# One core, a float32 mixer block: token-major products made 512 columns wide, gated linear attention in 64x64 tiles, and a new static order

## The chip, the cores and the metric

The kernel runs on one core of a Trainium2 chip. The metric is device time in microseconds (us) of one execution; lower is better. Engines are named as in the profile: PE is TensorE (matrix products and transposes), PEld its weight loads, DVE is VectorE, ACT is ScalarE, POOL is GpSimd, SP is SyncE, which issues most of the loads.

## The reference

Two layers, each with four token mixers that read the same normalised input: multi-head latent attention, neighbourhood attention, a long convolution (Hyena) and bidirectional gated linear attention (GLA). There are 256 context tokens and 256 latent tokens; the last layer needs no output for the context tokens. Everything is float32.

```python
for l in range(DEPTH):                                   # DEPTH = 2, D_MODEL = 1024
    h  = rms_norm(x,  pre_g[l]) * (1.0 + scale) + shift  # scale, shift from silu(c) @ ada_w[l]
    hc = rms_norm(cx, pre_g[l]) * (1.0 + scale_c) + shift_c
    ya, yca = mla_branch(h, hc, ...)                     # low-rank latents: rms_norm(h @ w_in[:, :256]) ...
    yb, ycb = na_branch(h, hc, ...)
    yh, ych = hyena_branch(h, hc, ...)
    yg, ycg = gla_branch(h, hc, ...)
    # merge_branches, for the latent and (layer 0 only) the context stream:
    gates  = sigmoid(h @ w_in[:, merge])                 # 4 branches x 1024 channels
    merged = sum(gates[i] * ((y[i] * silu(h @ w_in[:, z[i]])) @ w_branch[l, i]) for i in range(4))
    x = x + gate * rms_norm(merged @ w_out[l], post_g[l])
```

In the GLA, for each of 4 heads (key width 64, value width 128), 2 directions and chunks of 64 tokens: `a = tril((q*exp(b-bm)) @ (k*exp(bm-b)).T)`, `o = a @ v + (q*exp(b)) @ s`, and the state `s` goes on from chunk to chunk as `s = decay * s + k_out.T @ v`.

## The kernel before, in words

**Products.** Full float32 products are made of three in the faster type `fp32r`: every operand is split into a high and a low part (`wh`, `wl` of a weight; `hh`, `hl` of the normalised input; `gh`, `gl` of a gated branch output), and `mm3` issues high x high, high x low and low x high into the same PSUM bank. Products where both operands are plain float32 (the GLA, the Fourier products of the Hyena) stand in the trace as two records each. There are two kinds of projections. Channel-major ones (`proj_chan`, PSUM tile `pc`) load a piece of weights as the stationary operand and stream the tokens: 512 columns where both streams are wanted (layer 0), 256 where only one is (most of layer 1). Token-major ones (`tok`, PSUM tiles `pj` for the merge gates and the values, `br` for the branch products; `wo` of `project_out` and `pa` of the latents are built alike) hold 128 tokens stationary and stream weights: 256 columns at a time, 224 in `pa`.

**Weights.** `piece` brings 512 KB by SP into one of 3 `raw` buffers; ACT casts it to `wh` and DVE subtracts to give `wl`, each in two halves. The pool `wp` has 4 buffers of 1024 columns for each of `wh` and `wl`. A token-major call (`w_tok`) takes two pieces (8 k-tiles of 256 columns), so that two calls' weights fit.

**GLA.** `gla_dir` works on two heads (a head pair `p`) in one direction `r`, and is called four times in a layer. It makes scores (`atp`: per 128 tokens and head one 128x128x128 product, with the other head's rows of the query tile `qp` zeroed), masks them (`at`), makes state contributions (`kv`, 64x64 tiles), and sums `go` from `at` x values and from `qp` x state (`st`, output tiles of 64 tokens, again over all 128 rows). The decay logits `lg` are plain float32 products over 32 rows.

**Latents.** `latents` normalises the `pa` result of 128 tokens, turns it with four 128x128 transposes into one PSUM tile `lat` and one more transpose into `glrp`; both come from the pool `pt`, which has two banks. ACT and DVE empty `lat` in seven steps. The pool `pa` has four banks, `pmm` has two.

**Order.** PE's order is static: `drive` runs the parts of the kernel as coroutines on a counted clock (each product adds its columns/2400), and a part that issued work for another engine asks to be resumed after so many counted microseconds from the table `WAIT` (one number for each layer). What is ready by priority goes next. The other engines' orders are chosen when the program is built. The order on all engines is fixed then; at run time an engine waits where its next instruction isn't ready.

## Time and profile before

| | before |
|---|---|
| time, median of 3 runs | 1424.36 us (1422.72 to 1428.23) |
| the profiled execution's own time | 1426.96 us |
| its span, first to last instruction | 1425.2 us |
| PE busy | 1359.8 us, 95% |
| weight loads of PE busy | 1187.0 us, 83% |
| DVE, ACT, POOL busy | 889.0, 591.3, 339.7 us |
| HBM read | 163.19 MB |

The span is what the trace shows; the execution's own time is 1.8 us longer. Busy time is the union of instruction spans; since PE's products overlap each other in the pipeline (a record lasts longer than the step to the next one), what a stream of products costs is read from the starts of rows that follow each other, not from the mean duration of one.

### The profile page before, as it was taken

The page shows a single profiled execution, that of the slowest core. Times are in us where ns is not written, and L with a number is a line of the kernel's source. Part 1 is how long each engine was busy: PE and PEld are TensorE (multiplying, and loading weights), DVE is VectorE, ACT ScalarE, POOL GpSimd, SP SyncE. Part 2 cuts the span into 40 slices and gives each one's busy share as a digit, 9 for nine tenths or more (in the row PEclk, how much of TensorE's full clock was granted, in tenths as well). Part 3 has the DMA queues.
Part 4 walks back from the last instruction along what each step waited for, and adds up shares of the span by engine and source line. Part 5 has one row for each costly group of instructions (what it writes and reads, how often), then busy time and mean ns, then how long its engine had stood idle before and what let it go on. Part 6 is the DMA issues. An engine that isn't in the chain of part 4 may idle for free.

```text
span 1425.2 us, 24774 instructions
## 1 busy us (share of the span) xinstructions
PE 1359.8 (95%) x9852; PEld 1187.0 (83%) x9852; DVE 889.0 (62%) x1638; ACT 591.3 (41%) x1266; POOL 339.7 (24%) x438
## 2 busy tenths in 40 slices
PE   6989999999999999999999999889998999999996
PEld 3867788888997776889767999778888999899896
DVE  4668654565444447764476486966667776757764
ACT  3555453333222332222354443564545345434452
POOL 2423200152330201222111203532103331132110
PEclk9989999999999999999999999989998999999998
DMA  9421213232233432323334251432233255534361
GB/s 375 162 74 53 89 60 106 89 104 75 92 117 121 148 115 89 119 89 119 118 104 134 92 176 64 153 104 82 75 121 119 90 163 199 172 103 162 105 202 66
DMA packets 54308, 171.10 MB, mean 120 GB/s; under 512 B 7342, under 2 KB 10000, under 8 KB 54192
## 3 DMA queue, kind: packets, MB, share of 16 engines
q1 hardware_dynamic: 47904, 153.31, 32.3%
q0 software_dynamic: 5376, 15.90, 3.4%
q8 instruction: 77, 1.26, 0.3%
q10 hardware_dynamic: 912, 0.31, 0.1%
q14 instruction: 39, 0.32, 0.1%
HBM read 163.19 MB, written 6.31 MB: 119 GB/s over the span
## 4 chain that ended last, share of the span: by engine, by line
PE 44%; DVE 7%; issue 3%; DMA 2%; ACT 1%; POOL 1%; DVEq 0%; POOLq 0%; ACTq 0%
PE pj L380 14%; PE pc L380 9%; PE br L380 5%; PE wo L380 3%; DVE wl L370 2%; PE sc L380 2%; PE y L380 2%; DMA raw<-in_w_in 2%; PE pt L394 2%; PE pa L380 1%; PE yc L380 1%; DMA raw<-in_w_out 1%; PE go L380 1%; ACT wh L423 0%; PE q L380 0%
## 5 line engine op out<-in xcount | busy, mean ns | idle before, releaser
L370 DVE TENSOR_TENSOR wl<-raw,wh 128x512 fp32r<-128x512 f32 (+1 forms) x416 | 298.2, 751 | 205.4 <-ACT wh L423 200.1
L423 ACT CAST wh<-raw 128x512 fp32r<-128x512 f32 (+1 forms) x416 | 236.1, 616 | 325.2 <-DMA raw<-in_w_in 127.1
L380 PE MATMUL pj<-wh,hh 128*128 128x256 f32 x1024 | 302.4, 295 | 0.0
L380 PE MATMUL pj<-wl,hh 128*128 128x256 f32 x1024 | 290.5, 284 | 0.0
L380 PE MATMUL pj<-wh,hl 128*128 128x256 f32 x1024 | 290.4, 284 | 0.0
L380 PE MATMUL pc<-hh,wh 128*128 128x256 f32 (+1 forms) x688 | 244.0, 355 | 5.3 <-DVE zg L373 2.5
L380 PE MATMUL pc<-hh,wl 128*128 128x256 f32 (+1 forms) x688 | 231.2, 336 | 0.0
L380 PE MATMUL pc<-hl,wh 128*128 128x256 f32 (+1 forms) x688 | 230.9, 336 | 0.0
L380 PEld LDWEIGHTS pj<-wh,hh 128*128 128x128 f32 x1024 | 196.9, 192 | 17.8 <-issue 16.4
L380 PEld LDWEIGHTS pj<-wl,hh 128*128 128x128 f32 x1024 | 197.2, 193 | 2.9 <-issue 2.2
L380 PEld LDWEIGHTS pj<-wh,hl 128*128 128x128 f32 x1024 | 197.0, 192 | 0.0
L380 PEld LDWEIGHTS pc<-hh,wh 128*128 128x128 f32 x688 | 132.5, 193 | 30.2 <-issue 13.5
L380 PEld LDWEIGHTS pc<-hl,wh 128*128 128x128 f32 x688 | 132.6, 193 | 14.1 <-issue 3.1
L380 PEld LDWEIGHTS pc<-hh,wl 128*128 128x128 f32 x688 | 132.3, 192 | 13.4
L380 PE MATMUL br<-wh,gh 128*128 128x256 f32 x384 | 110.4, 288 | 0.0
L380 PE MATMUL br<-wh,gl 128*128 128x256 f32 x384 | 108.7, 283 | 0.0
L380 PE MATMUL br<-wl,gh 128*128 128x256 f32 x384 | 108.6, 283 | 0.0
L370 POOL TENSOR_TENSOR gl<-y,gh 128x256 fp32r<-128x256 f32 (+1 forms) x44 | 35.3, 806 | 279.9 <-ACT gh L405 279.9
L806 ACT ACTIVATE p<-sc,mx 128x512 f32<-128x512 f32 (+1 forms) x96 | 58.9, 615 | 55.9 <-DVE mx L804 50.8
L380 PEld LDWEIGHTS br<-wh,gh 128*128 128x128 f32 x384 | 73.6, 192 | 4.9 <-issue 3.7
L380 PEld LDWEIGHTS br<-wh,gl 128*128 128x128 f32 x384 | 73.6, 192 | 0.1
L380 PEld LDWEIGHTS br<-wl,gh 128*128 128x128 f32 x384 | 73.6, 192 | 0.0
(282 smaller groups left out, 2395.4 us busy)
## 6 DMA issues: line engine op xcount, KB each, us to landing
raw<-in_w_in SPq DMA_DIRECT2D x160, 512.0 KB, 3.5
adaw<-in_ada_w SPq DMA_DIRECT2D x44, 512.0 KB, 3.9
raw<-in_w_branch SPq DMA_DIRECT2D x32, 512.0 KB, 3.5
raw<-in_w_out SPq DMA_DIRECT2D x16, 512.0 KB, 3.5
H<-filt POOLq DMA_DIRECT2D x16, 256.0 KB, 3.6
nab<-in_na_bias POOLq DMA_DIRECT2D x16, 256.0 KB, 3.0
raw<-in_w_in SPq DMA_DIRECT2D x8, 448.0 KB, 3.4
x<-in_xin SPq DMA_DIRECT2D x4, 512.0 KB, 5.0
```

Source lines behind the costliest of these rows:

```text
L370: eng.tensor_tensor(out=out, in0=a, in1=b, op=ALU.subtract)
L380: self.nc.tensor.matmul(out, lhsT, rhs, start=start, stop=stop, skip_group_check=skip)
L394: self.nc.tensor.transpose(out, in_, self.ident)
L423: nc.scalar.copy(hi, raw[:, sl])
L806: nc.scalar.activation(p[h][:, :nk], ps[h][:, :nk], AF.Exp, bias=mx, scale=1.0, accum_out=sm)
```

## The change

- Token-major products stream 512 columns instead of 256 (`pa` of layer 0: 448 instead of 224). A weight piece holds 2 k-tiles of 512 columns; a `w_tok` call now takes four pieces. `wp` becomes 8 buffers of 512 columns for each of `wh` and `wl`, the same bytes, given back one k-tile at a time.
- In `gla_dir`, scores are made in 64x64 tiles: only the blocks of 64 tokens on the diagonal, each head on its own 64 rows and in its own PSUM bank. The products of query and state use 64 rows and 64 output tokens. The zeroed query tiles and their memsets go. Masking is done by four calls on 64 partitions instead of two (layer 0) or one (layer 1).
- The decay logits become one `fp32r` product over 96 rows (high, high and low parts stacked).
- The `lat` transposes write to the pool `pa` of four banks; ACT makes its four copies of them one after the other, and DVE's three follow.
- The mean of squares is scaled in the Square activation, and one DVE instruction adds the halves and the epsilon (`rstd_of`), in place of a DVE add and a POOL multiply-add.
- The table `WAIT` has new numbers, and one transpose step of the norm of the second stream stands ahead of a wait that it stood behind.

```diff
 WAIT = {
-    "latents": (10.5, 12.0),
-    "latents_out": (4.21, 0.7),
+    "latents": (10.0, 12.0),
+    "latents_out": (5.62, 0.49),
...
-    "gla_dir": (10.24, 4.0),
+    "gla_dir": (6.79, 4.0),
...
-        self.wp = pool("wp", 4)
+        self.wp = pool("wp", 8)
...
+    def rstd_of(self, halves):
+
+        m, r = self.t(1, "ms"), self.t(1, "rstd")
+        self.ts(m, halves[:, 0:1], halves[:, 1:2], ALU.add, EPS, ALU.add)
+        self.nc.gpsimd.tensor_tensor(out=r, in0=m, in1=self.mhalf[:, :1], op=ALU.pow)
+        return r
...
-            parts = [self.wp.tile([P, 1024], F32R, tag=tag, name=self.name(tag)) for tag in ("wh", "wl")]
-            parts = [(t[:, : k * n // 2], t[:, k * n // 2 : k * n]) for t in parts]
         out = []
+        m = k * n // 2
         for f in range(2):
-            hi, lo = (p[f] for p in parts)
-            sl = slice(f * k * n // 2, (f + 1) * k * n // 2)
+            if spare:
+                hi, lo = (t[:, :m] for t in self.pair(self.s, "w"))
+            else:
+                hi, lo = (self.wp.tile([P, 512], F32R, tag=tag, name=self.name(tag))[:, :m] for tag in ("wh", "wl"))
+            sl = slice(f * m, (f + 1) * m)
             nc.scalar.copy(hi, raw[:, sl])
             self.sub(nc.vector, lo, raw[:, sl], hi.bitcast(F32))
...
-    def w_tok(self, l, name, c, n=256):
-
-        return self.rows([self.w_in(l, name, 2 * c + i, 4, n) for i in range(2)])
+    def w_tok(self, l, name):
+
+        return self.rows([self.w_in(l, name, i, 2, 512) for i in range(4)])
...
-    def tok(self, w, lhs, nk, s, base):
-
-        ps = self.ps(self.pmm, base, (P, 2, 256))
-        for i in range(2):
-            for kt in range(nk):
-                self.mm3(ps[:, i, :], lhs(s, kt, i * P, i * P + P), w(kt), kt == 0, kt == nk - 1)
-                if kt % 2:
-                    yield 0
+    def tok(self, w, lhs, nk, s, i, base):
+
+        ps = self.ps(self.pmm, base)
+        for kt in range(nk):
+            self.mm3(ps, lhs(s, kt, i * P, i * P + P), w(kt), kt == 0, kt == nk - 1)
+            yield 0
         return ps
...
-        pp = self.ps(self.pt, "lat", (P, 4, P))
+        pp = self.ps(self.pa, "lat", (P, 4, P))
...
-                self.mm(ps, wg[:32, r, p, :], self.glrT[:32, :])
+
+                self.mm(ps, wg[:96, r, p, :], self.glrT[:96, :])
...
+        ps = [self.ps(self.pa, "atp", (P, 4, CHUNK)) for _ in range(2)]
+        at = [self.T("at", (P, 4, P)) for _ in range(2)]
+        for h in range(2):
+            nc.gpsimd.memset(at[h][:, t0:], 0.0)
+        for tt in tts:
+            for h in range(2):
+                rows = slice(64 * h, 64 * h + 64)
+                for cc in range(2):
+                    t = slice(tt * P + 64 * cc, tt * P + 64 * cc + 64)
+                    self.mm(ps[h][64 * cc : 64 * cc + 64, tt, :], kt_[rows, t], qt[rows, t], cost=0.035)
...
+        for tt in tts:
+            for h in range(2):
+                self.mm(po[h][:, tt, :], at[h][:, tt, :], v(tt, (2 * p + h) * P, (2 * p + h) * P + P), tt == t0, False, skip=True)
...
-                    for h in range(2):
-                        self.mm(po[64 * cc : 64 * cc + 64, i, h, :], qp[h][:, c * CHUNK : c * CHUNK + CHUNK], st[c], False, True, skip=True)
...
+                    rows = slice(64 * h, 64 * h + 64)
+                    self.mm(po[h][64 * cc : 64 * cc + 64, tt, :], qt[rows, c * CHUNK : c * CHUNK + CHUNK], st[c][rows], False, True, skip=True, cost=0.06)
...
     def merge_gates(self, l, i, c, outs):
-        w = self.w_tok(l, f"merge{2 * i + c // 2}", c % 2)
+        w = self.w_tok(l, f"merge{2 * i + c}")
         gates = {}
         for s in outs:
-            ps = yield from self.tok(w, self.hT, KT, s, "pj")
-            gates[s] = self.G("gt", (P, 2, 256))
-            self.nc.scalar.activation(gates[s], ps, AF.Tanh, scale=0.5)
+            for t in range(2):
+                ps = yield from self.tok(w, self.hT, KT, s, t, "pj")
+                gates[s, t] = self.G("gt")
+                self.nc.scalar.activation(gates[s, t], ps, AF.Tanh, scale=0.5)
         return gates
```

The order of the built programs shows what this does on the engines. First PE in layer 0, where the latents are turned, before (a number behind a name tells the buffer; `x4` is four equal rows):

```order
L380 MATMUL pc_885<-hh_268,wl_880 128x512
L394 MATMUL lat_904<-ident,xt_741 128x128 x4
L394 MATMUL glrp_916<-ident,kr_742 32x128
L394 MATMUL lat_919<-ident,xt_755 128x128 x4
L394 MATMUL glrp_931<-ident,kr_756 32x128
L394 MATMUL lat_934<-ident,xt_769 128x128 x4
L394 MATMUL glrp_946<-ident,kr_770 32x128
L394 MATMUL lat_949<-ident,xt_786 128x128 x4
L394 MATMUL glrp_961<-ident,kr_787 32x128
L380 MATMUL pc_885<-hh_268,wh_879 128x512
```

The same place in the changed program:

```order
L386 MATMUL pc_813<-hh_288,wl_810 128x512
L400 MATMUL lat_829<-ident,xt_661 128x128 x4
L400 MATMUL glrp_841<-ident,kr_662 96x128
L400 MATMUL lat_845<-ident,xt_676 128x128 x4
L400 MATMUL glrp_857<-ident,kr_677 96x128
L400 MATMUL lat_861<-ident,xt_691 128x128 x4
L400 MATMUL glrp_873<-ident,kr_692 96x128
L400 MATMUL lat_877<-ident,xt_709 128x128 x4
L400 MATMUL glrp_889<-ident,kr_710 96x128
L386 MATMUL pc_813<-hh_288,wh_809 128x512
```

The order of the eight steps is the same, with no other product between them; what differs is the pool that the four `lat` tiles come from, and that each `glrp` has 96 rows.

Second, PE in a GLA direction of layer 0, the sum `go` of one half of the tokens, before:

```order
L380 MATMUL go_3411<-gla_v_1926,at_3299 128x128 x4
L380 MATMUL go_3411<-st_3282,qp_3162 64x128
L380 MATMUL go_3411<-st_3282,qp_3163 64x128
L380 MATMUL go_3411<-st_3282,qp_3162 64x128
L380 MATMUL go_3411<-st_3282,qp_3163 64x128
L380 MATMUL go_3411<-st_3282,qp_3162 64x128
L380 MATMUL go_3411<-st_3282,qp_3163 64x128
```

In the changed program (the last two products with `at` and the first with the state; the other half of the tokens follows without a break):

```order
L386 MATMUL go_3036<-gla_v_2193,at_2903 128x128
L386 MATMUL go_3037<-gla_v_2193,at_2904 128x128
L386 MATMUL go_3036<-st_2884,qp_2771 64x128
L386 MATMUL go_3037<-st_2884,qp_2771 64x128
L386 MATMUL go_3036<-st_2884,qp_2771 64x128
L386 MATMUL go_3037<-st_2884,qp_2771 64x128
L386 MATMUL go_3036<-st_2884,qp_2771 64x128
L386 MATMUL go_3037<-st_2884,qp_2771 64x128
```

Products of the two heads alternate between two PSUM banks and between the two halves of the rows; one direction now makes all its `at` products and then all its state products, once, where it did so twice in layer 0.

Third, ACT in layer 1 at the merge gates of the Hyena branch (`gt` is a gate, from a finished `pj`; each `wh` CAST needs its `raw` piece landed and a free `wp` buffer), before:

```order
L423 CAST wh_13409<-raw_13407 128x512 x2
L1304 ACTIVATE gt_13338<-pj_13267 128x512
L423 CAST wh_13417<-raw_13415 128x512 x2
L423 CAST wh_13484<-raw_13482 128x512 x2
L1304 ACTIVATE gt_13405<-pj_13356 128x512
L423 CAST wh_13492<-raw_13490 128x512 x2
```

And in the changed program:

```order
L1336 ACTIVATE gt_11736<-pj_11689 128x512
L435 CAST wh_11767<-raw_11765 128x512
L435 CAST wh_11771<-raw_11765 128x512
L435 CAST wh_11777<-raw_11775 128x512
L435 CAST wh_11781<-raw_11775 128x512
L435 CAST wh_11787<-raw_11785 128x512
L435 CAST wh_11791<-raw_11785 128x512
L1336 ACTIVATE gt_11763<-pj_11738 128x512
L435 CAST wh_11797<-raw_11795 128x512
L435 CAST wh_11801<-raw_11795 128x512
L1336 ACTIVATE gt_11838<-pj_11805 128x512
```

Before, two pieces of weights stood between two gates, all along; now the eight casts of the next call's weights stand together, from the last gate but one of a call to the first of the next.

## Rows read from the trace of the kernel before

**Rows 1.** The page: busy time of each engine, share of the span.

```profile
PE 1359.8 (95%) x9852; PEld 1187.0 (83%) x9852; DVE 889.0 (62%) x1638; ACT 591.3 (41%) x1266; POOL 339.7 (24%) x438
```

**Rows 2.** PE's groups of instructions, shapes apart: xcount | busy us, mean ns | idle.

```profile
L380 PE MATMUL pj<-wh,hh 128*128 128x256 f32 x1024 | 302.4, 295 | 0.0
...
L380 PE MATMUL br<-wh,gh 128*128 128x256 f32 x384 | 110.4, 288 | 0.0
...
L380 PE MATMUL wo<-wh,mh 128*128 128x256 f32 x96 | 29.2, 304 | 0.0
...
L380 PE MATMUL atp<-qp,ktl 128*128 128x128 f32 x96 | 14.6, 298 | 0.0
...
L380 PE MATMUL go<-st,qp 128*64 128x128 f32 x176 | 13.5, 281 | 0.0
...
L380 PE MATMUL lg<-glrT,wg 32*128 32x512 f32 x16 | 9.0, 640 | 0.0
```

**Rows 3.** Timeline of PE, layer 1: first and 36th of a run of 256-column products.

```profile
1226.27 0.28 PE L380 MATMUL pj<-wh,hh 128*128 128x256 f32 x1
...
1230.47 0.28 PE L380 MATMUL pj<-wh,hl 128*128 128x256 f32 x1
```

**Rows 4.** Timeline of PE, layer 0: first and 12th of a run of 512-column products.

```profile
319.38 0.39 PE L380 MATMUL pc<-hh,wh 128*128 128x512 f32 x1
...
321.88 0.39 PE L380 MATMUL pc<-hh,wl 128*128 128x512 f32 x1
```

**Rows 5.** Timeline of PE in layer 0's GLA; the second row is the first's last record.

```profile
307.83 1.05 PE L380 MATMUL go<-gla_v,at 128*128 128x128 f32 x8
...
308.61 0.28 PE L380 MATMUL go<-gla_v,at 128*128 128x128 f32 x1
...
308.81 1.09 PE L380 MATMUL go<-st,qp 128*64 128x128 f32 x12
309.83 1.37 PE L380 MATMUL kv<-gla_v,kT 64*64 64x128 f32 x28
311.13 1.16 PE L380 MATMUL atp<-qp,ktl 128*128 128x128 f32 x8
```

**Rows 6.** Timeline where layer 0's latents are turned; idle time and releaser in brackets.

```profile
73.00 0.60 PE L394 MATMUL lat<-ident,xt 128*128 128x128 f32 x4
...
73.64 0.37 ACT L904 ACTIVATE cqT<-lat,par 128x128 fp32r<-128x128 f32 x1 [0.85 <-PE lat L394]
...
76.42 1.02 PE L394 MATMUL lat<-ident,xt 128*128 128x128 f32 x4 [2.70 <-ACT rotT L906]
...
83.01 0.63 PE L380 MATMUL pc<-hl,wh 128*128 128x512 f32 x1
83.43 0.63 PE L380 MATMUL pc<-hh,wl 128*128 128x512 f32 x1
```

**Rows 7.** PE's waits by releaser: total us, times, longest.

```profile
PE lat L394 <- ACT rotT L906: 8.3, 2, 5.5
...
PE lat L394 <- ACT glrT L909: 1.7, 3, 0.9
```

**Rows 8.** Windows: length, PE busy, granted clock (PEclk), DMA share, GB/s.

```profile
76.60:86.80 10.20, 8.09 (x25) 0.50 0.11 37
943.50:950.30 6.80, 5.45 (x26) 0.50 0.27 79
1226.00:1294.00 68.00, 68.00 (x531) 1.00 0.44 144
```

**Rows 9.** The page: groups of the weights' subtraction and cast, and a piece's load.

```profile
L370 DVE TENSOR_TENSOR wl<-raw,wh 128x512 fp32r<-128x512 f32 (+1 forms) x416 | 298.2, 751 | 205.4 <-ACT wh L423 200.1
L423 ACT CAST wh<-raw 128x512 fp32r<-128x512 f32 (+1 forms) x416 | 236.1, 616 | 325.2 <-DMA raw<-in_w_in 127.1
...
raw<-in_w_in SPq DMA_DIRECT2D x160, 512.0 KB, 3.5
```

**Rows 10.** Timeline of POOL at the end of the program.

```profile
1417.12 0.19 POOL L400 TENSOR_SCALAR ms<-ss 128x1 f32<-128x1 f32 x1 [10.67 <-DVE ss L367]
```

More of the change, by code (lines that the diff above doesn't have):

```diff
@@ L1168, in gla @@
         yield self.wait("gla_decay")
[L1169 removed]
+        o = [self.S("glao", (P, 4, P)) for _ in range(4)]
         for p in range(2):
@@ new lines, in gla_dir @@
+        for h in range(2):
+            for cc in range(2):
+                rows = slice(64 * cc, 64 * cc + 64)
+                nc.vector.copy_predicated(at[h][rows, t0:, 64 * cc : 64 * cc + 64],
+                                          self.causal[rows, r, 64 * cc : 64 * cc + 64].unsqueeze(1).to_broadcast([64, len(tts), 64]),
+                                          ps[h][rows, t0:, :])
+        yield self.wait("gla_at")
+        yield self.wait("gla_scores")
+        po = [self.ps(self.pa, "go", (P, 4, P)) for _ in range(2)]
@@ L1339, in project_out @@
         nc, d = self.nc, self.d
-        ws = {c: self.rows([self.piece(d["w_out"][l, 2 * c + i], 4, 256, c > 1) for i in range(2)]) for c in (2, 3, 0, 1)}
+        ws = {half: self.rows([self.piece(d["w_out"][l, half, j], 2, 512, half == 1) for j in range(4)]) for half in (1, 0)}
         for s in streams:
@@ L1392, in layer @@
         self.cqT = [self.pair(self.s, "cqT"), self.pair(self.s, "cqT")]
-        self.ckvT, self.rotT, self.glrT = self.pair(self.s, "ckvT"), self.S("rotT"), self.S("glrT")
+        self.ckvT, self.rotT, self.glrT = self.pair(self.s, "ckvT"), self.S("rotT"), self.s.tile([P, 512], F32R, tag="s", name=self.name("glrT"))
         lats = []
-        ws = ws or [self.w_tok(l, "A", c, 224) for c in (1, 0)]
+        if l == 0:
+            w = self.rows(ws)
+            ws = lambda c: w
+        else:
+            halves = {c: self.rows(self.w_latent(l, (2 * c, 2 * c + 1))) for c in (1, 0)}
+            ws = halves.get
         for g in ((0, 1),) if l == 0 else ((1,), (0,)):
@@ L1454, in layer @@
         yield from self.na_qk(l, outs, qs, ks)
-        gates = yield from self.gate_list(l, 1, range(4), outs)
+        gates = yield from self.gate_list(l, 1, range(2), outs)
         yield lambda: na.done
@@ L1479, in merge_list @@
             w = self.branch_w(l, i, c)
-            for s in gates[c]:
-                yield from self.merge_one(w, s, c, gates[c][s], ys, merged, first)
+            for s, t in gates[c]:
+                yield from self.merge_one(w, s, t, c, gates[c][s, t], ys, merged, first)
     def main(self):
@@ L1495, in ada @@
                     pieces[j, part, half] = self.ada_load(0, part, j, half, alloc(half))
-        early = lambda half: [self.wp.tile([P, 1024], F32, tag=("wh", "wl")[half], name=self.name("adaw"))]
+        early = lambda half: [self.wp.tile([P, 512], F32, tag=("wh", "wl")[half], name=self.name("adaw")) for _ in range(2)]
         xt = {}
@@ L1511, in main @@
         loaded.append(self.filter_in(0, 1))
-        first = [self.rows([first[c, i] for i in range(2)]) for c in (1, 0)]
         def later():
```

261 lines of the change are left out of this document (125 added, 136 removed).

## The prediction

> **What bounds the kernel now.** I read the page first: PE is busy 1359.8 of 1425.2 us [rows 1], so only what shortens PE's stream or closes its gaps can move the end. PE's waits come next: of the 65 us of the span in which it is not busy (the first load and the tail behind the last product among them), the largest item that isn't start or end is the turning of the latents, 8.3 + 1.7 us over both layers [rows 7]. The window over the merge gates of layer 1 says the same from near: PE is busy 68.00 of 68.00 us there [rows 8]. So I cost PE's stream by the steps between the starts of neighbouring rows, and then ask what the new order waits for.
>
> **Wider products.** A run of 256-column products in layer 1 starts at 1226.27 and its 36th at 1230.47: 4.20/35 = 0.120 us each [rows 3]. Twelve 512-column products in the channel-major code start from 319.38 to 321.88: 2.50/11 = 0.2273 us [rows 4]. Two of 256 cost 0.240, so joining a pair saves 0.0127 us. The pairs: `pj` has three groups of 1024, `br` three of 384, `wo` as many as six groups of 96 [rows 2]: 3072 + 1152 + 576 = 4800 products, 2400 pairs, 30.5 us. `pa` in layer 0 goes from 192 products of 224 columns (4 token tiles, 2 halves, 8 k-tiles, 3) to 96 of 448. On the line through the two steps 224 columns take 0.107 and 448 take 0.2005, 0.013 less than two of them; by 512's price a pair saves nothing. I take 1.3. **-31.8 us**, between -30.5 and -32.
>
> Here a page of the Trainium skill bears on the sum. "TensorE: Matmul & The Clock Gate", section "Back-to-back issue gap", gives a step of columns/2.4 GHz plus 2.5 ns for an isolated stream; by it a pair would save 2.5 ns and this part 6 us. The rows disagree: 0.120 is 13 ns over 256/2.4 = 107, and 0.2273 is 14 ns over 213, so the fixed part here is five times that and is what the pair saves once.
>
> **Decay logits.** `lg` is busy 9.0 us in 16 records [rows 2]; eight `fp32r` products of 512 columns at 0.2273 are 1.8, and if each stands alone with the 0.39 of its row [rows 4], 3.1. **-6.5 us** (-5.9 to -7.2). The extra row copy and subtraction in `wg` and `glrT` lie on ACT and DVE at 41% and 62% busy [rows 1]; not covered, `glrT`'s subtraction would cost eight times some 0.3.
>
> **GLA tiles.** `atp` is busy 14.6 us for 48 products, `go` from `st` 13.5 for 88 [rows 2]. No row shows 64x64 products of the new shapes; the nearest is `kv`, 64x64 tiles of 128 columns: 14 products from 309.83 to 311.13, 0.093 each, while `go` from `st` took 308.81 to 309.83 for 6, 0.17 each [rows 5]. The new `go` has 88 products of `kv`'s shape: 8.2 us at 0.093. `kv` mostly has two of the four tiles in work at once, the new order four in a row (two heads by two halves), so half of it, 4.1, is the lower bound. The new `atp` has 96 products of half the columns: 4.5 at half of 0.093, 8.9 at the whole. So the two fall from 28.1 to between 8.6 and 17.1; I take 14 us saved, as four distinct tiles in a row are nearer to the lower bound. The upper bound is no overlap at all: 88 times 0.17 and 96 times 0.093 are 23.9, which still saves 4. **-14 us** (-4 to -19.5). Masking costs DVE 32 calls in place of 12; the part that waits (`gla_scores`) has other products in between. If that cover is gone, some 0.4 us for each of eight directions.
>
> A rule that speaks against the tiles is in "TensorEngine Tiling (Array Packing)", section "Key Properties": a change of the tiling mode drains the engine. The trace agrees: the eight `at` records start from 307.83 to 308.61, 0.11 apart, and the first `st` follows at 308.81, 0.20 on [rows 5]. By it the change pays nothing more, since `go` changes shape as often per direction, or once instead of twice in layer 0, and `kv` to `atp` no longer does.
>
> **Latents.** In layer 0 the second `lat` starts 2.70 us after PE went idle, for ACT's last copy out of the first [rows 6]; in both layers such waits come to 10 us [rows 7]. With four banks no `lat` waits for another. What is left is `glrp` in two banks: its third waits for ACT to empty the first, and ACT then has 5 copies for each tile, each at most the 0.37 of the first, against PE's 0.60 for a `lat` [rows 6]. Two such waits of about 1 us stay in layer 0, none in layer 1, where only two tiles follow each other: -8 us. With it goes the clock: from 76.6 to 86.8 and from 943.5 to 950.3 the granted clock is 0.50, that is 1.2 in place of 2.4 GHz [rows 8], each time at the waits for the latents, and the products after it step by 0.42 instead of 0.227 us [rows 6]. Those 17 us cost up to 8.5. Layer 0 keeps some idle time, so I count half. **-12 us** (0, if a `lat` tile waits as long for a bank of `pa`, to -18.5).
>
> **Norm chains.** POOL's multiply-add, 0.19 us and its hand-over, goes from the tail [rows 10], and the new DVE step takes the old one's place. 0.3 at the end, and as much at two or three points between the layers. **-1 us** (0 to -2).
>
> **Weights at the hand-over.** This is the new wait. A call of `w_tok` now fills `wp`; the next call's eight casts can begin only as its last pass goes through the k-tiles, 3 x 0.2273 = 0.68 us each, 5.45 for the pass. Three of the four next pieces already stand in `raw`. The fourth is issued when the first is cast and subtracted: two k-tiles 1.36, cast and subtraction 0.62 + 0.75, load 3.5, then 0.62 + 0.75 again [rows 9]: 7.6 us, and its first k-tile is wanted at 5.45 + 6 x 0.68 = 9.5. Two us are left. Queued behind the casts on ACT are the last gate of the call and `go`'s copies; a cast that comes late on DVE (0.75 of each 0.68 us, beside 62% other work averaged) uses them up. Five calls in each layer follow straight upon another. I take 0.4 us for each of ten: **+4 us** (0 to +25). In layer 0, `ada` loads hold a `raw` buffer too and eat the slack first.
>
> **The rest of the order** has new numbers everywhere. PE's idle time outside the latents, 65 - 10 = 55 us with start and tail, could grow or shrink; I see no reason for a sign: 0, between -10 and +10.
>
> Sum: -31.8 - 6.5 - 14 - 12 - 1 + 4 = -61.3. The profiled execution took 1426.96 us, its span 1425.2; 1426.96 - 61.3 = 1365.7. It lies 2.6 above the median of the runs, 1424.36, so the median should come to **1363 us**. A measurement of this kernel tells about 0.5%, 7 us, from no change.
>
> **Rivals.**
> *Starved hand-overs (slower).* If the chain of load, cast and subtraction stood in the open at each of the 20 `w_tok` calls, 3.5 + 0.62 + 0.75 = 4.9 us each, 98 us would replace the 4: 1363 + 94 = 1457. It decides from 65/20 = 3.3 us per call on. For it: `wp` holds one call instead of two. Against: the three pieces in `raw`, the release by k-tile, DMA at a share of 0.44 in that stretch [rows 8]. 4 in 100 for slower by 0.5%, and 4 for the same.
> *Half-starved.* One to two us at each call, 20 to 40 us: 1379 to 1399. 13 in 100.
> *Only the wide products pay.* The tiles run without overlap (+10), `lat` waits for `pa`'s banks, which the filters and scores use as well (+12), the new order idles 10 more: 1395. 8 in 100.
> *The clock falls in the GLA.* Tiles leave much of the array unused; if the clock went to half in each of eight directions as it did from 943.5 on [rows 8], 6.8 us with 3.4 lost each, 27 us come back: 1390. 6 in 100; the `kv` tiles of before run between products at full clock.
> *The wide products don't pay.* If with tokens as the stationary operand 512 columns step by twice 0.120, since `pc`'s rows have the weights there, the pairs bring nothing: 1363 + 32 = 1395. 2 in 100: 128x128 operands are loaded for each product either way. By the Trainium skill's rule above, 6 of the 32 would still come.
> *As summed:* 1346 to 1379, 58 in 100. *Better*, with all clock and idle time back: below 1346, 5 in 100.
>
> The range that leaves out 2 in 10 at most goes from 1346 to 1392. Faster by over 0.5%: 0.92; within: 0.04; slower: 0.04.
>
> **What would show it.** `pj`, `br` and `wo` rows of 512 columns at steps of 0.227; no `lat` wait over 1 us, and a clock of 1.00 after the latents; `atp` and `go` busy under 15 us together (without the `at` products); PE idle between two `pj` calls, released by DVE `wl` or ACT `wh`, below 0.5 us each. The prediction is wrong if those last gaps reach 2 us, or if PE's idle time as a whole grows over the 65 us of before.

## The result and the profile after

| | before | after |
|---|---|---|
| time, median (runs) | 1425.34 us (1422.72 to 1428.23) | 1392.89 us (1391.00 to 1394.17) |
| ratio, 95% interval | | 0.9771 (0.9748 to 0.9794) |
| the profiled execution, its span | 1426.96, 1425.2 us | 1392.82, 1391.0 us |
| PE busy, not busy within the span | 1359.8, 65.4 us | 1310.1, 80.9 us |

The change saved 32 us; 61 were forecast. The time lies 0.9 us above the range. PE's busy time fell by 49.7 us, but PE's idle time grew by 15.5 us, and this is the sign that the prediction named for being wrong ("if PE's idle time as a whole grows over the 65 us of before").

The page's first line, which answers to [rows 1]:

```profile
PE 1310.1 (94%) x7444; PEld 1033.3 (74%) x7444; DVE 901.3 (65%) x1676; ACT 603.4 (43%) x1268; POOL 320.2 (23%) x408
```

PE's groups, shapes apart, which answer to [rows 2] (count, busy us, mean ns, idle and releaser):

```profile
L386 PE MATMUL pj<-wh,hh 128*128 128x512 f32 x512 | 212.8, 416 | 3.1 <-DVE zg L379 1.6 <-ACT wh L435 1.5
L386 PE MATMUL br<-wh,gh 128*128 128x512 f32 x192 | 79.1, 412 | 5.0 <-DVE merged L379 2.6 <-DVE gt L379 2.4
...
L386 PE MATMUL atp<-qp,ktl 64*64 64x64 f32 x192 | 7.4, 232 | 0.0
L386 PE MATMUL go<-st,qp 64*64 64x128 f32 x176 | 7.0, 279 | 0.0
L386 PE MATMUL lg<-glrT,wg 96*128 96x512 f32 x8 | 3.2, 396 | 0.0
```

PE's timeline: two ends of a run of 30 `pj` products (compare [rows 3, 4]), and a GLA direction of layer 0 (compare [rows 5]):

```profile
298.24 0.73 PE L386 MATMUL atp<-qp,ktl 64*64 64x64 f32 x26
298.90 2.05 PE L386 MATMUL go<-gla_v,at 128*128 128x128 f32 x16
300.88 1.09 PE L386 MATMUL go<-st,qp 64*64 64x128 f32 x28
305.56 0.64 PE L386 MATMUL ada<-adaw,sv 128*32 128x256 f32 x8 [3.59 <-issue]
...
1043.07 0.39 PE L386 MATMUL pj<-wh,hh 128*128 128x512 f32 x1
...
1049.64 0.39 PE L386 MATMUL pj<-wh,hl 128*128 128x512 f32 x1
```

(1049.64 - 1043.07)/29 = 0.2266 us a step, the price of [rows 4]. `go` with the state starts 28 records within 1.09 - 0.28 = 0.81 us, 0.030 each, and a product is two records: 0.06 us where [rows 5] had 0.17; `atp` has 0.018 a record. `atp` and `go` from `st` are busy 14.4 us together; the prediction had asked for less than 15.

The latents of layer 0, where two waits of 2.70 and 0.90 us stood [rows 6, 7], and the windows (as in [rows 8], but with the busy time of PE, PEld, DVE, ACT and POOL in turn, each with its number of instructions, before the clock):

```profile
77.11 0.60 PE L400 MATMUL lat<-ident,xt 128*128 128x128 f32 x4
80.47 0.32 PE L400 MATMUL glrp<-ident,kr 128*96 128x128 f32 x1 [2.76 <-DVE glrT L376]
...
81.56 0.63 PE L386 MATMUL pc<-hl,wh 128*128 128x512 f32 x1
81.99 0.63 PE L386 MATMUL pc<-hh,wl 128*128 128x512 f32 x1
```
```profile
81.20:84.60 3.40, 3.40 (x11) 2.63 (x10) 2.84 (x7) 2.64 (x9) 0.00 (x0) 0.50 0.06 24
...
1057.40:1071.10 13.70, 7.75 (x57) 6.33 (x58) 9.53 (x17) 5.70 (x12) 4.63 (x9) 0.50 0.13 40
1196.00:1264.00 68.00, 67.82 (x310) 53.95 (x309) 52.19 (x75) 27.95 (x48) 18.26 (x18) 1.00 0.45 144
```

No `lat` waits any more. One `glrp` does, the third, and the clock is at its lower level for 3.4 us behind it in place of 10.2; in layer 1 no `lat` or `glrp` waits. But a new stretch at 0.50 stands at 1057.40, in layer 1's GLA. PE's waits say what stands there (total us, times, longest; compare [rows 7]):

```profile
PE ktp L400 <- DVE ktl L370: 10.3, 1, 10.3
...
PE ada L386 <- issue: 4.9, 2, 3.6
PE adat L386 <- ACT h L662: 4.4, 3, 1.9
...
PE ht L400 <- DVE xn L383: 3.1, 3, 1.4
PE glrp L400 <- DVE glrT L376: 2.8, 1, 2.8
...
PE br L386 <- DVE merged L379: 2.6, 1, 2.6
PE br L386 <- DVE gt L379: 2.4, 2, 2.0
...
PE pj L386 <- ACT wh L435: 1.5, 1, 1.5
```

**Where the 34 us between the two spans came from.** I summed PE's rows of each trace by output tile: the step from a row's start to the next row's start, with idle time before a row kept apart (us):

| tiles | steps before | after | difference | idle before | after |
|---|---|---|---|---|---|
| `pj`, `br`, `wo`, `pa` | 640.9 | 617.3 | -23.6 | 4.4 | 14.7 |
| `go`, `atp`, `kv` | 48.4 | 33.0 | -15.4 | 0.0 | 1.0 |
| `lg` | 8.4 | 1.9 | -6.5 | 0.0 | 0.0 |
| `lat`, `glrp` | 7.5 | 3.9 | -3.6 | 11.0 | 2.8 |
| `ktp` | 3.4 | 3.7 | +0.3 | 3.4 | 11.6 |
| `ada`, `adat`, `ht` | 50.6 | 53.1 | +2.5 | 9.5 | 15.9 |
| `pc` | 373.8 | 371.8 | -2.0 | 5.3 | 7.4 |
| all others, start and tail | 243.3 | 242.4 | -0.9 | 15.3 | 10.5 |
| all | 1376.3 | 1327.1 | -49.2 | 48.9 | 63.9 |

So most of the work came off PE as priced: the first four lines are -49.1 where the prediction had -31.8 - 14 - 6.5 and some 4 of the clock, and the 7 us between them are the wide products', 23.6 in place of 31.8. Outside the latents, idle time went from 37.9 to 61.1 us, +23.2, where the prediction had +4 for the weights and 0 for the rest: 10.3 more before the token-major tiles, 8.2 before `ktp`, 6.4 before `ada`, `adat` and `ht`. That is the question for the experiments: which part of the change brings these waits.

### The profile page after: what moved, and what is told of

Same layout as the page of the kernel before. It is cut to its first block, busy times and chain, and to the rows that moved or that the text cites. A ratio compares the mean times of both kernels' runs of the same rounds, so it can differ in the third digit from the quotient of the medians.

```text
span 1391.0 us, 20163 instructions
## 1 busy us (share of the span) xinstructions
PE 1310.1 (94%) x7444; PEld 1033.3 (74%) x7444; DVE 901.3 (65%) x1676; ACT 603.4 (43%) x1268; POOL 320.2 (23%) x408
## 4 chain that ended last, share of the span: by engine, by line
PE 40%; DVE 7%; issue 3%; ACT 3%; DMA 2%; POOL 1%; DVEq 0%; POOLq 0%; ACTq 0%
PE pc L386 11%; PE pj L386 10%; PE br L386 5%; PE wo L386 3%; PE sc L386 2%; PE y L386 2%; DVE wl L376 2%; PE pt L400 2%; DMA raw<-in_w_out 1%; PE pa L386 1%; ACT wh L435 1%; PE yc L386 1%; DMA raw<-in_w_in 1%; DVE ub L370 0%; PE go L386 0%
## 5 line engine op out<-in xcount | busy, mean ns | idle before, releaser
L386 PE MATMUL pc<-hh,wh 128*128 128x256 f32 (+1 forms) x688 | 242.4, 352 | 7.4 <-DVE cv L379 3.4
L386 PE MATMUL pj<-wh,hh 128*128 128x512 f32 x512 | 212.8, 416 | 3.1 <-DVE zg L379 1.6
L386 PE MATMUL pj<-wl,hh 128*128 128x512 f32 x512 | 200.2, 391 | 0.4 <-DVE wl L376 0.4
L386 PE MATMUL pj<-wh,hl 128*128 128x512 f32 x512 | 200.2, 391 | 0.0
L386 PEld LDWEIGHTS pc<-hl,wh 128*128 128x128 f32 x688 | 132.2, 192 | 14.3 <-issue 2.6
L386 PEld LDWEIGHTS pj<-wh,hh 128*128 128x128 f32 x512 | 96.2, 188 | 33.3 <-issue 12.0
L386 PEld LDWEIGHTS pj<-wh,hl 128*128 128x128 f32 x512 | 96.1, 188 | 21.1
L386 PEld LDWEIGHTS pj<-wl,hh 128*128 128x128 f32 x512 | 96.5, 188 | 20.2 <-issue 2.6
L386 PE MATMUL br<-wh,gh 128*128 128x512 f32 x192 | 79.1, 412 | 5.0 <-DVE merged L379 2.6
L386 PE MATMUL br<-wl,gh 128*128 128x512 f32 x192 | 76.7, 399 | 0.0
L386 PE MATMUL br<-wh,gl 128*128 128x512 f32 x192 | 76.4, 398 | 0.0
L820 DVE TENSOR_REDUCE mx<-sc 128x1 f32<-128x512 f32 (+1 forms) x96 | 55.1, 592 | 11.4 <-PE sc L386 10.5
```

What stands on the lines that cost most here:

```text
L386: self.nc.tensor.matmul(out, lhsT, rhs, start=start, stop=stop, skip_group_check=skip)
L820: nc.vector.tensor_reduce(out=mx, in_=ps[h][:, :nk], axis=AX.X, op=ALU.max, negate=True)
```

## Experiments

Times are medians. A ratio is to the kernel before, run beside it, with its 95% interval (about 0.2% to either side, 3 us); "against the changed kernel" is the difference of two such ratios times 1425 us, so that 4 us are not much more than nothing. Of a longer edit the fence shows one place. The theory at the start (T1) was that the work came off as priced and the new numbers of `WAIT` opened new waits; the rivals were that the waits come from the structure (T2), or that the products pay less than priced (T3).

**The old table** (`e1`): the whole table of before in the changed kernel.

```diff
-    "gla_decay": (7.1, 2.9),
+    "gla_decay": (7.1, 9.2),
...
-    "hy_product": (13.35, 11.95),
+    "hy_product": (9.0, 11.95),
```

> The changed kernel with the whole WAIT table of the kernel before; everything else as changed. Theory 1 (the work came off as priced, and the new numbers of the table opened new waits and half-clock stretches that ate about 25 us): PE busy stays about 1310, PE's not-busy time falls from 81 us to 50 to 65, the 10.3 us wait of ktp for DVE's ktl in layer 1 is under 2 us, time 1365 to 1383. Theory 2 (the new waits come from the structure: one call's weights in wp, more masking calls, longer runs on ACT): not-busy time stays at 75 to 90 us, time 1387 to 1399. In between or slower than 1399: the old numbers open other waits of their own, and the table has to be taken entry by entry.

1399.8 us, 0.9828 (0.9808 to 0.9848): 8 us slower than the changed kernel. That is the third case of the expectation: `ktp` waits only 3.0 us for `ktl`, but other waits open, and PE's time not busy stays at 82 us. T1 falls as it was stated: the new numbers are worth 8 us to this code.

**One number** (`e2`): only `gla_decay` of layer 1 goes back, so that more products stand ahead of the `ktp` that waits 10.3 us.

```diff
-    "gla_decay": (7.1, 2.9),
+    "gla_decay": (7.1, 9.2),
```

> The changed kernel with one number of the table, gla_decay of layer 1, back from 2.9 to the 9.2 of before. Theory 1: the first ktp of layer 1's GLA moves behind more products; its 10.3 us wait for DVE's ktl goes to under 2 us, and the 13.7 us at half clock that begin within it go too, worth 3 to 5 us more: 1377 to 1383. Theory 2 (DVE and ACT are late there whatever PE does first): the wait stays over 5 us or comes up at the next instruction, 1389 to 1396.

1393.51 us, 0.9769 (0.9746 to 0.9791): no change. The wait for `ktl` shrank to 3.3 us, but one of the products put ahead of it, a `br`, now waits 2.9 us for a gate on ACT. From the last `lg` to the branch products of the GLA it is 79.4 us (1043.4 to 1122.8) after 80.6 (1042.1 to 1122.7). What PE does first hardly matters there; what it waits for is late, as the second theory had it.

**Products in halves** (`e3`): the wide products of `tok` and `project_out` issued as two of 256 columns, with weights, order and waits as changed.

```diff
-            self.mm3(ps, lhs(s, kt, i * P, i * P + P), w(kt), kt == 0, kt == nk - 1)
+            for c in range(2):
+                cs = slice(c * 256, c * 256 + 256)
+                self.mm3(ps[:, cs], lhs(s, kt, i * P, i * P + P), [x[:, cs] for x in w(kt)], kt == 0 and c == 0, kt == nk - 1)
```

> The changed kernel with each 512-column token-major product of the gates, values, branches and the output projection issued as two of 256 columns, one behind the other; order, weights and waits as changed. By the prediction's step 0.0127 us for each of 2400 pairs comes back: +30.5 us, 1418 to 1428, PE busy about 1340. Rival (the wide products are worth less at the end, since they also shorten what covers ACT's and DVE's work): PE busy rises by 30 but the not-busy time falls from 81 to about 65, time 1405 to 1412.

1410.3 us, 0.9900 (0.9881 to 0.9918): 18 us slower; the width is worth 18 us at the end. The time lies in the rival's range, but the rival's mechanism is not what the page shows:

```profile
PE 1331.5 (94%) x9844; PEld 1167.1 (83%) x9844; DVE 900.7 (64%) x1676; ACT 603.7 (43%) x1268; POOL 320.6 (23%) x408
```

PE's busy time rises by 21.4 us, not by 30, and its time not busy in the span of 1409.7 is 78.2, 2.7 less than in the changed kernel, where the rival had some 16 less. So little of the width's worth went into waits; it took less off PE than was priced. That is T3, for this part.

**Latents in two banks** (`e4`):

```diff
-        pp = self.ps(self.pa, "lat", (P, 4, P))
+        pp = self.ps(self.pt, "lat", (P, 4, P))
```

> The changed kernel with the turned latents back in the pool of two banks. By the prediction's latents step, 8 us of PE's waits come back (one of about 2.7 and two of about 1 us are left of them now) and half of the clock's 8.5: 1401 to 1406, with lat waiting for ACT's or DVE's emptying for 6 to 10 us and 10 us or more at half clock in layer 0 in place of 3.4. Rival (the clock is what PE's idle time elsewhere makes of it and the latents bring only their waits): 1398 to 1401.

1397.66 us, 0.9808 (0.9786 to 0.9831): 5 us. `lat` waits again, 6.8 us for DVE's `ckvT` and 2.8 for ACT's `wukv`, and the 2.8 of `glrp` are gone: 6.8 more, of which 5 reach the end. The clock did stay low for longer behind the latents of layer 0, at 0.50 for 10.2 us from 79.3 as was expected and not for 3.4; but 5 us, to within some 4, is no more than the waits, and leaves nothing that the clock's share could be read from.

**GLA in whole rows** (`e5`): `gla_dir` and the sums of `gla` as before, with the new logits.

```diff
-                    self.mm(ps[h][64 * cc : 64 * cc + 64, tt, :], kt_[rows, t], qt[rows, t], cost=0.035)
+                    self.mm(ps[:, i, h, :], kt_[:, tt * P : tt * P + P], qp[h][:, tt * P : tt * P + P])
```

> The changed kernel with the GLA's scores, masking, state products and copies in the form of before (128 rows, zeroed query tiles, twice per direction in layer 0); decay logits, wide products, latents and table as changed. The prediction's step: the tiles save 14 us (4 to 19.5), so 1403 to 1410. Theory now (T4: work that comes off PE is only partly given back at the end, since the unchanged or longer chains on ACT and DVE stand out of it as waits; the two-halves run gave back 17 of about 26 us): 8 to 10 us of PE busy time come back but part of them fills waits, 1396 to 1402, PE's not-busy time falls from 81 to 75 or less. Rival (the extra masking calls cost what the tiles save): 1390 to 1395.

1409.24 us, 0.9880 (0.9858 to 0.9903): 16 us, and PE's busy time rises by 16.7 to 1326.8. The tiles were priced at 14, and they pay in full; the theory of that moment, that each saved microsecond is only partly given back, missed here.

**Logits in float32** (`e6`):

```diff
-                self.mm(ps, wg[:96, r, p, :], self.glrT[:96, :])
+                self.mm(ps, wg[:32, r, p, :], self.glrT[:32, :])
```

> The changed kernel with the decay logits as plain float32 products over 32 rows; without the row copies and subtractions that the stacked form needs on ACT and DVE. The prediction's step: 6.5 us come back, 1399 to 1400. T4: the faster logits only start a chain on DVE, ACT and POOL that is as long as before, and in layer 1 PE then waits 10.3 us for it: about half, 1395 to 1397, and glrp's wait of 2.8 us in layer 0 shrinks.

1394.85 us, 0.9790 (0.9768 to 0.9812): 3 us for the 6.5 that PE has less to do, hardly clear of the interval. `ktp` then waits 5.4 us in place of 10.3, and a `kv` waits 3.7: earlier logits mostly start the wait earlier.

**Gates behind the logarithms** (`e7`), and with `gla_decay` as well (`e8`). In layer 1's GLA of the changed kernel the end of the decay chain looks like this, on ACT, on POOL and on PE:

```profile
1050.70 1.28 ACT L1192 ACT_TABLE_LOAD   x1
1051.99 1.67 ACT L1192 ACTIVATE ee<-ee 128x512 f32<-128x512 f32 x3
1053.67 1.28 ACT L1336 ACT_TABLE_LOAD   x1
1054.97 0.60 ACT L1336 ACTIVATE gt<-pj 128x512 f32<-128x512 f32 x1
1055.58 1.28 ACT L1192 ACT_TABLE_LOAD   x1
1056.88 0.63 ACT L1192 ACTIVATE ee<-ee 128x512 f32<-128x512 f32 x1
...
1061.00 0.61 ACT L1249 ACTIVATE ktl<-gb 128x512 f32<-128x512 f32 x1
```
```profile
1057.59 1.27 POOL L376 TENSOR_TENSOR mn<-mn,ee 128x512 f32<-128x512 f32 x1 [0.26 <-ACT ee L1192]
1058.80 0.66 POOL L1238 COPY bm<-gb 128x8 f32<-128x8 f32 x1
```
```profile
1042.14 0.40 PE L386 MATMUL lg<-glrT,wg 96*128 96x512 f32 x1
...
1062.40 1.12 PE L400 MATMUL ktp<-ident,ktl 128*128 128x128 f32 x4 [10.33 <-DVE ktl L370]
```

From the last `lg` to `ktp` it is 20 us. Three logarithms run, then a merge gate (`gt`, a Tanh) with a table load ahead of it and another behind it, then the fourth logarithm; POOL's fourth subtraction waits for that, and the `bm` of the first direction stands behind the subtraction on POOL, though it needs nothing of it. The Trainium skill ("ScalarE: Activation LUTs", section "Rules for kernel authors") asks to do all of one table set before a switch; this is such a place. The same page of the Trainium skill gives, in its section "What ACT_TABLE_LOAD costs", 1283 ns for the load, which the 1.28 of these rows bear out, and 1380 ns more of draining, which they do not: the load of 1050.70 ends at 1051.98, and the next ACTIVATE starts at 1051.99.

```diff
+                with self.tc.issue_after(self.last_ln) if self.last_ln is not None else nullcontext():
+                    self.nc.scalar.activation(gates[s, t], ps, AF.Tanh, scale=0.5)
```

> The changed kernel with one more order on ACT: a merge gate issued after the GLA's logarithms comes behind the last of them, so that in layer 1 no Tanh stands between them and two of the four table loads of 1.28 us go. T4, with ACT as the engine behind layer 1's GLA wait: ktp's wait of 10.3 us falls by 3 to 4.5 us and the time by 2 to 5: 1388 to 1391. Rival (DVE's weight subtractions or POOL set that wait): the wait stays at 9 to 10.5 us, 1392 to 1394.

> Both edits at once: gla_decay of layer 1 back at 9.2, so that 30 or so products stand in front of the first ktp, and the gates behind the logarithms on ACT. With the number alone the time did not move, since a br then waited 2.9 us for the gate that stood behind a table load, merged 4.4 and ktl 3.3. If ACT's order is the common cause, these three waits shrink to under 5 us together: 1384 to 1389. If the chain is just as long whatever the order, 1391 to 1395.

1390.53 us, 0.9754 (0.9733 to 0.9775), and 1389.57 us, 0.9749 (0.9729 to 0.9768): 2 and 3 us, `e8` at the edge of what was expected (its text puts the 4.4 us for `merged` beside the others; they stand in layer 0, at 286.9, and have nothing to do with it). In `e7` the wait of `ktp` falls from 10.3 to 1.9 us, but a `br` waits 6.1 and a `kv` 3.1. In `e8` the four logarithms stand together, and the two gates wait instead, and PE for them:

```profile
1049.34 2.19 ACT L1193 ACTIVATE ee<-ee 128x512 f32<-128x512 f32 x4
1051.54 1.28 ACT L1339 ACT_TABLE_LOAD   x1
1052.84 1.09 ACT L1339 ACTIVATE gt<-pj 128x512 f32<-128x512 f32 x2
```
```profile
1053.49 0.79 PE L387 MATMUL br<-wh,gh 128*128 128x512 f32 x1 [6.10 <-ACT gt L1339]
```

So ACT's order is part of this wait, and only a part of it can be had by turning it round.

**Halves of the change** (`e9`, `e10`): before with the wide products, their weights and the norm's edit alone, and before with the tiles, logits and latents alone; both with the old table.

```diff
-        return self.rows([self.w_in(l, name, 2 * c + i, 4, n) for i in range(2)])
+        return self.rows([self.w_in(l, name, i, 2, 512) for i in range(4)])
```

> Of the change only the wide token-major products with their weights in four pieces and wp of eight buffers (and the norm's chains with the moved transpose step); the GLA, the decay logits, the latents and the whole WAIT table as before. By the prediction's terms -31.8 + 4 - 1: 1396. By the steps read from the changed kernel's trace (512 columns 0.2285 on average, not 0.2273) -26 on PE's stream, and by the two-halves run 17 of that at the end: 1404 to 1410 (T4). If the parts hinder one another rather than other engines (that is, the wide products alone are worth their whole 26): 1396 to 1401.

> The kernel before with the GLA tiles, the decay logits and the latents of the change, its narrow products, its weights, its norm and its table. By the prediction's terms -14 - 6.5 - 12: 1392. By the runs that undid one part each, -16 (tiles), -2.5 (logits), -5 (latents): 1401. T4 (waits of ACT and DVE chains come out when PE gets shorter): 1400 to 1408. With the wide-only run it tells whether the two halves of the change add up to the whole's 32 us, or to more, which would mean that both run into the same waits.

1424.15 us, 0.9994 (0.9975 to 1.0013): the wide products, which were the largest term of the prediction, come to nothing together with their weights and the norm's edit. 1399.99 us, 0.9829 (0.9808 to 0.9850): the others pay 24 us. Every expectation missed `e9`, by 14 us at least; `e10` came out as the runs that undid one part each had it, 1401. The halves do not hinder each other: their 1 + 24 us are, within the intervals, the 24.5 of `e1`, the whole change with the same table. What lies between 25 and 33 is the new table.

**The norm** (`e11`, `e13`; `e12` and `e16` with `e8` besides). The change let the second stream's norm issue the first transposes of `ht` ahead of its wait for the adaptive scale. At the start of the program PE then does this (changed kernel; then `e13`, where only that step is back in its place):

```profile
10.77 3.50 PE L386 MATMUL ada<-adaw,sv 128*32 128x256 f32 x16 [2.17 <-DMA adaw<-in_ada_w]
15.67 0.48 PE L400 MATMUL ht<-ident,xn 128*128 128x128 f32 x1 [1.40 <-DVE xn L383]
17.45 0.90 PE L400 MATMUL ht<-ident,xn 128*128 128x128 f32 x3 [1.30 <-DVE xn L383]
...
31.31 0.72 PE L386 MATMUL pa<-wh,hh 128*128 128x448 f32 x1
```
```profile
15.24 0.61 PE L386 MATMUL adat<-par,rows 128*128 128x2 f32 x4 [1.25 <-DVE rows L591]
...
22.53 1.97 PE L400 MATMUL ht<-ident,xn 128*128 128x128 f32 x8
...
26.42 0.47 PE L386 MATMUL pa<-wh,hh 128*128 128x448 f32 x1
```

In the first, four transposes stand ahead of everything that the first stream needs and wait twice for DVE's `xn`; the first `pa` starts at 31.31. In the second it starts at 26.42. Over the whole kernel the rows of `ada`, `adat` and `ht` take 50.6 us of steps and 10.8 of idle time in `e13`, against 53.1 and 15.9 in the changed kernel: 7.6 us between them.

```diff
-            if s == 0 and self.abq[l] <= q:
+            if self.abq[l] <= q:
                 yield lambda: self.abq[l] > q
                 yield self.wait("norm_ab")
...
-            if self.abq[l] <= q:
-                yield lambda: self.abq[l] > q
-                yield self.wait("norm_ab")
```

> The changed kernel with the norm of before: its longer chain, and no transpose step of the second stream ahead of a wait. By the prediction the chains save 1 us: 1393 to 1395. The traces' starts speak against it: the first pa starts 3.5 us later in the changed kernel (31.3 for 27.8), behind two waits of ht for xn of 1.4 and 1.3 us that were not there, since the step moved ahead stands before the products that the first stream needs: 1389 to 1391, and the first pa at 28 to 29.

> The changed kernel with three edits: gla_decay of layer 1 back, gates behind the logarithms on ACT, and the norm of before. If the start's 2 to 3 us add to the 3 of the other two: 1386 to 1388. If the start's gain is lost at a later wait: 1388 to 1391.

> The changed kernel with the second stream's first transpose step back behind its wait; the shorter chain of the norm stays. If the moved step is what cost 6.7 us: 1384 to 1387, first pa at 27 to 28. If the chain itself costs (its one DVE step is later than the old pair): 1390 to 1393.

> The changed kernel with gla_decay of layer 1 back, the gates behind the logarithms, and the transpose step back behind its wait, the short norm chain kept. If the chain saves its 1 us: 1382 to 1384, against 1384 with the whole norm of before. If the chain costs: 1385 to 1390.

`e11` (the whole norm of before) 1386.15 us, 0.9723 (0.9702 to 0.9744); `e13` (only the step) 1383.82 us, 0.9722 (0.9702 to 0.9742). Both are 7 us faster than the changed kernel, more than the start alone had suggested: the moved step is the cause, and the short chain neither costs nor saves anything that these runs could tell. `e12` 1383.98 us, 0.9708 (0.9689 to 0.9728), and `e16` 1381.83 us, 0.9705 (0.9686 to 0.9723), the fastest version of all: 9 us faster than the changed kernel, 42 us faster than before.

**The wide products without the norm's edit** (`e14`), and with the new table as well (`e15`):

> The wide products alone, with the norm of before as well: GLA, logits, latents, norm and table of before. If the 6.7 us of the norm's edit add: 1416 to 1419. If the wide products' loss lies all in their own structure and order: 1422 to 1426. By the two-halves run (17 us): 1407 to 1409, which would say that nothing else takes from them.

> As the kernel before it, with the WAIT table of the change. If the table was fitted to the wide products' shorter calls: 6 to 12 us faster than with the old one. If it was fitted to the rest, or the wide products lose by their weights: the same within 3 us, or slower.

1417.95 us, 0.9958 (0.9942 to 0.9974), and 1418.8 us, 0.9952 (0.9933 to 0.9971). The norm's edit adds up (0.9994 to 0.9958 is 5 us), and the new table brings these products nothing. Alone they pay 6 us with their weights, where `e3` gave 18 for the width, with the weights' new order kept. `e14`'s groups show what came with them:

```profile
L386 PE MATMUL pj<-wl,hh 128*128 128x512 f32 x512 | 201.0, 393 | 2.6 <-DVE wl L376 2.6
...
L386 PE MATMUL br<-wh,gh 128*128 128x512 f32 x192 | 78.5, 409 | 2.4 <-DVE gt L379 1.2 <-ACT wh L435 1.1
L386 PE MATMUL br<-wl,gh 128*128 128x512 f32 x192 | 76.6, 399 | 4.1 <-DVE wl L376 4.1
```

[Rows 2] have no idle time ahead of `pj` and `br`. Here it is 9.1 us in these three groups, and 7.8 of them wait for a weight's cast or subtraction: the hand-over, over the price of 4. In the changed kernel itself, with the new table and the other parts, all such waits of `pj` and `br` are 1.9 us.

**Without DVE's subtractions** (`e17` changed, `e18` before):

```diff
-                hi, lo = (self.wp.tile([P, 512], F32R, tag=tag, name=self.name(tag))[:, :m] for tag in ("wh", "wl"))
+                hi = lo = self.wp.tile([P, 512], F32R, tag="wh", name=self.name("wh"))[:, :m]
...
-            self.sub(nc.vector, lo, raw[:, sl], hi.bitcast(F32))
+            if spare:
+                self.sub(nc.vector, lo, raw[:, sl], hi.bitcast(F32))
```

> The changed kernel without the low parts of the streamed weights: the 416 subtractions on DVE are left out (some 300 us of its 901 busy) and the high part stands in the place of the low one, so PE issues the same products. If DVE's load is what turns PE's saved time into waits: PE's not-busy time falls from 81 us to 50 to 62, the ada, merged, gt and ktl waits shrink, time 1360 to 1375, and the distance to the kernel before with the same edit is 42 to 52 us. If ACT, the loads and the order are the cause: 1380 to 1392, distance 28 to 36.

> The kernel before with the same edit: no low parts of the streamed weights, 416 subtractions fewer on DVE, the same products on PE. PE waited for DVE there in only some 15 of 65 us, and the 8 us of the latents are ACT's: 1412 to 1421 whichever cause holds; it is the base for the distance.

1363.74 us, 0.9579 (0.9554 to 0.9605), and 1403.77 us, 0.9849 (0.9825 to 0.9873). The high part stands in the place of the low one here, so that PE issues the same products. The time of `e17` lies in the range for DVE as the cause; but the kernel before gained as well, so the distance decides. It is 2.70% or 38 us, between the two expectations, and its growth from 32.6 is hardly beyond the intervals. The kernel before gained 21 us where at most 14 were expected. Pages of `e17` and `e18`, and `e17`'s longest wait:

```profile
PE 1299.8 (95%) x7444; PEld 1029.3 (75%) x7444; DVE 624.1 (46%) x1260; ACT 602.3 (44%) x1268; POOL 303.5 (22%) x408
```
```profile
PE 1351.6 (96%) x9852; PEld 1183.0 (84%) x9852; DVE 619.3 (44%) x1222; ACT 589.1 (42%) x1266; POOL 319.4 (23%) x438
```
```profile
PE ktp L400 <- DVE ktl L370: 9.6, 1, 9.6
```

PE's time not busy is 1366.4 - 1299.8 = 66.6 us in `e17` and 1404.0 - 1351.6 = 52.4 in `e18`: 14.3 and 13.0 less than with the subtractions, so DVE takes about as much from both kernels. And the 10 us wait stays, with a third of DVE's work gone. DVE's load is not the main thing that turned the change's gain into waits: by these runs it accounts for some 6 of the 29 us that are missing, hardly clear of nothing. The question was put too broadly.

## Why the prediction was wrong

From ratios to the time before, turned into us; what a part is worth is what the run that undid it lost, unless said otherwise:

| term | predicted | on PE's stream | at the end |
|---|---|---|---|
| wide products | -31.8 | -23.6 | -18 (`e3`) |
| GLA tiles | -14 | -15.4 | -16 (`e5`) |
| decay logits | -6.5 | -6.5 | -3 (`e6`) |
| latents | -12 | -3.6 and 8.2 of waits | -5 (`e4`) |
| norm | -1 | | +7 (`e11`, `e13`) |
| weights at the hand-over | +4 | | some +12 (`e14` less `e3`, an estimate) |
| rest of the order | 0 | | -8 for the table (`e1`) |
| sum | -61.3 | | -31; measured -33 |

That the sum comes near the measured time proves little: the lines were taken in different surroundings, each is good to some 4 us, and the +12 is no run of its own.

**The steps that failed.** By size the first is the price of the wide products, the term of -31.8: they brought 18 us at the end (`e3`). By kind the plainest is the norm term, which costs moved code at nothing. The text of the change had said that a transpose step of the second stream stands ahead of a wait that it stood behind; the prediction's "norm chains, -1" counted the shorter chain and left the moved step out of the sum. It cost 7 us (`e13`). That alone would have brought the time into the range, and it is a quarter of the 29 us by which the forecast missed. The order of PE's rows at the start, which could be had, would have shown four `ht` in front of the first stream's first `adat`. The other failing terms are the clock's share of the latents, the logits, and the weights.

**Wide products.** The step of 0.227 was right in a quiet run, but not as a mean: over all `pj` products whose step isn't disturbed by a wait, 512 columns average 0.2288 and 256 columns 0.1197, so a pair saves 10.6 ns, not 12.7. 2400 pairs are 25 us; the lower clock takes some 2 of them (13.2 us of these tiles' steps at 0.50 after, 8.4 before). The trace of `e3` says the same from the other side: against the changed kernel these tiles' steps are 23.0 us longer, all other steps 1.6 shorter and PE's idle time 2.6 less, 18.7 together, which is the distance of the two profiled executions.

**Weights at the hand-over** had the right place, but its size is not shown. The two microseconds of slack worked out there did not hold with the old table: `e14` shows 7.8 us of waits for casts and subtractions, and the difference of `e14` and `e3` says 12 with what follows from them (a difference of two runs in different surroundings). In the changed kernel itself they look otherwise: `pj` waits 1.5 us once for `wh`, over the 0.5 that was named and under the 2, and 0.4 for `wl`, less than was priced; but `ada` waits 3.59 and 1.3 under "issue". SP's queue shows why: the load of `adaw` for 305.56 is issued at 300.61, behind `raw` loads that wait for DVE's `wl`, and itself into a buffer from which the last `wl` is made at 300.58. That "`ada` loads hold a `raw` buffer too and eat the slack first" was right. The rival "half-starved", 1379 to 1399, holds the measured time, but by luck: one to two us at each of 20 calls is not what the waits show.

```profile
287.04 8.53 SPq L426 DMA_DIRECT2D raw<-in_w_in  x2
300.61 0.33 SPq L548 DMA_DIRECT2D adaw<-in_ada_w  x1
```

**Latents.** The 8 us of waits left as the prediction said, down to one `glrp` wait of 2.76 (two of about 1 were expected, for ACT; it is for DVE's `glrT`). The half of the clock's price did not come back: the clock stayed up behind the latents but for 3.4 us, where the price had been read from 17, but steps at 0.50 add up to 30.1 us before and 32.9 after over the whole kernel. The clock fell at other waits instead, the longest time at 1057.40.

**Decay logits** came off PE to the tenth, and are worth about half: in layer 1 they start a chain of 20 us over DVE, ACT and POOL that PE waits for. That the chain was as long before could be read in the old trace: from the last `lg` to the first `ktp` it is 1069.0 to 1092.5 there, with 156 products between, where the changed kernel has 42.

**GLA tiles** were right, within the bounds on PE and at the end: `atp` and `go` take 12.6 us less, and `kv`, which was not counted, 2.8. The wait for the masks did not come. "The clock falls in the GLA" was right once, in layer 1, but within the wait of 10.3 us and not in the tiles.

**The rest of the order** was costed at 0 with no reason for a sign. The numbers of the table turned out worth 8 us to the code that they came with, and nothing to the wide products alone (`e15`). PE's idle time outside the latents, which the prediction kept at 55 us but for the 4 of the weights, grew by 23 all the same; where it grew is listed under the table of tiles, and no single run takes it all back.

Still open: why the mean step of 512 columns lies above that of the quiet run; how much of the layer 1 wait could be had with another order on ACT and POOL (`e7`, `e8`, `e12` and `e16` each gained 2 to 3 us by it); and how much of the estimated 12 us is hand-over alone, since no run changed the weights' order by itself. A larger `wp` was not tried.

## What to carry to other kernels

Price every line of a change that moves an instruction, above all a line that moves one ahead of a wait on the engine that bounds the kernel: here one transpose step cost over a third of what the best part of the change brought. Price a stream by the mean step over the whole trace, not by one quiet run: a difference of two steps loses most by it, 10.6 ns for 12.7 here. When products on the bound get shorter, list the chains on the other engines that they covered, with their length in the old trace and the products that stand beside them; what is left uncovered can come back as a wait, as with the logits (the GLA tiles, by contrast, paid in full), and reordering the bound engine moved such a wait here without removing it. And say with a part's value what came with it: the wide products are 18 us by their width alone, 6 with their weights' new order and the old table, 1 with the norm's edit besides.

## What was not expected of the hardware

The step of a 512-column product varies more at full clock than that of 256 columns: 0.2266 from 1043.07 to 1049.64, 0.2288 in the mean of `pj`; 256 columns have a median of 0.120 and a mean of 0.1197. Why was not looked into. Four 64x64 tiles in turn start a record every 0.030 us with 128 columns and every 0.018 with 64, against 0.17 a product, two records, for 128 rows and 64 outputs [rows 5].
